# A hybrid decoder step in which the build-time scheduling pass is given another timing model

## The chip, the cores and the metric

One of the eight cores of a Trainium2 chip runs the whole step as one program. The metric is device time in microseconds (us), the median of several runs; a profiled execution gives the trace. TensorE multiplies matrices, VectorE (DVE) and ScalarE (ACT) do elementwise work, GpSimd (POOL) a little of it, and SyncE (SP) issues most transfers. Each engine takes its own queue of instructions in the order in which it was written.

## The reference

Two layers run over 320 tokens (256 of a prompt, 64 of eight sample sequences), with 1024 features, everything in float32:

```python
def layer(x, p, lw, h0, cache_k, cache_v):
    x = x + 0.5 * swiglu(rms_norm(x, lw['ffn1_norm']), ...)      # 1024 -> 2816 -> 1024
    mix, new_k, new_v, h_last = token_mixer(rms_norm(x, lw['mix_norm']), lw, h0, cache_k, cache_v)
    x = x + mix
    x = x + 0.5 * swiglu(rms_norm(x, lw['ffn2_norm']), ...)
    gate = jax.nn.sigmoid((rms_norm(x, lw['ple_norm']) @ lw['ple_w_gate']).astype(F32))
    x = x + ((p @ lw['ple_w_proj']).astype(F32) * gate).astype(x.dtype)

def token_mixer(h, lw, h0, cache_k, cache_v):
    z = h @ lw['w_in']                       # -> u (512) | q (512) | k (128) | v (128)
    y_ssm, h_last = ssm_scan(u, h0, ...)     # h_t = Abar h_{t-1} + Bbar u_t, 32 groups, 64 complex states each
    y_attn = attn_prompt(...) or attn_sample(...)   # window of 128 keys, one sink for each head
    y = jnp.concatenate([rms_norm(y_ssm, ...), rms_norm(y_attn, ...)], axis=-1)
    return y @ lw['w_out'], new_k, new_v, h_last
```

A final RMSNorm follows. The new keys and values and the last states are outputs too.

## The kernel before

Features lie on the 128 partitions, tokens along the rows, so the residual `x` is eight tiles of 128x320. A float32 product is done as three products of rounded parts (`mm3`, L177 to L187): weight and operand are each split into a rounded half (`wh`, `xh`) and a remainder (`wl`, `xl`), and L181, L182 and L183 accumulate wh*xh, wh*xl and wl*xh. One weight block of 1024 columns thus gives 24 matmuls against eight feature blocks.

Weights come in one long order (`weight_order`). `wfetch` loads a block through SP into one of four `wr` buffers (L158), ScalarE rounds it into `wh` (L162), VectorE subtracts to get `wl` (L163); there are four buffers of `wh` and of `wl` (`WB`). `wtake` keeps two blocks fetched ahead (`PF`) in the source.

A layer is a feed-forward part (`ffn`: gate and up products, L287 to L295, down products, L326 to L337), the token mixer (`mix`), a second `ffn` and the layer-input part (`ple`). In layer 0 the tables of the state-space scan for both layers are made beside the two `ffn` (`prep`), and `step` holds these instructions behind a recent weight split, a recent GpSimd instruction and a recent transfer with `tc.issue_after`.

The mixer's units are written in the order that `MIXSEQ` lists: `p` are projections (L577; evacuated by VectorE at L596, L600 or L603), `i` turns a quarter of u into chunks (L607: transposes L613 and L618, products L624, with copies by ScalarE between), `h` is the scan on VectorE (L647 to L685: steps `astep` at L639 to L645, the fix-up at L678 to L683), `v` transposes the values (L701), `s`, `f` and `m` are scores (L725 for the prompt), transposes (L750) and value products (L759) of attention, `y` are the outputs of the scan (L844, L855), `z` the layer-input projections, which need nothing of the mixer, `t` and `w` load tables of the scan (L567), `g` is a gate product, `A` and `S` the output projections. In the middle it reads

```python
... i1 p8 h0 t1 p9 v t2 p5 t0 e x p4 y0 s0 s1 w2 f0 p6 m0 p7 s2 f1 t3 m1 s3 f2 m2 y0 w3 y0 y1 s4 ...
```

That source order is not yet the order of the queues. When the `with _tile.TileContext(...)` block in `_build` closes, a scheduling pass plays the traced program against a model of the machine. As soon as an engine is free in the model it is given, of the instructions that are ready there (inputs made, a buffer of their pool free), the one that comes first in the source. The order found in this way is written out as the engine's queue and stays fixed on the chip. Named edges such as those of `issue_after` are kept.

Of the kernel before, what the change touches and what calls it, by code (L numbers as in the profile page):

```python
# [49 lines left out]
def hybrid_step_kernel(ctx: ExitStack, tc, I, O):  # L50
    nc = tc.nc
# [14 lines left out]
    def nm(s):  # L66
        uid[0] += 1
        return f"{s}_{uid[0]}"
# [7 lines left out]
    def pst(tag):  # L76
        return pp_.tile([P, 512], F32, name=nm(tag), tag=tag, bufs=PBUFS[tag])
# [4 lines left out]
    def cp(out, in_):  # L82
        S.activation(out, in_, AF.Copy)

# [1 line left out]
    ident = cpool.tile([P, P], F32, name="ident")  # L86
    make_identity(nc, ident)
    ones = cpool.tile([P, 1], F32, name="ones")
# [18 lines left out]
    def gcol(l, off, m):  # L107
        c = l * NPRM + off + m
        return prm[:, c : c + 1]

# [1 line left out]
    seq = MIXSEQ.split()  # L112
    def weight_order():
        for l in range(L):
# [72 lines left out]
                    waiting.pop(0)[1]()  # L187

    class Norm:
        """Statistics and split operand of an RMSNorm over nb feature blocks."""  # L190

        def __init__(self, nb, gain, split=True, pre=1.0):
            self.nb, self.gain, self.split, self.pre = nb, gain, split, pre
# [41 lines left out]
            ]  # L235

        def finish(self, then=None):
            """Statistics of the row scale; its broadcast is left for later, behind a few products."""
            ps = pst("pa")
            for c, t0 in enumerate(STAT):  # L240
                sums = [self.acc] + self.sums
                for i, a in enumerate(sums):
                    PE.matmul(ps[:SN, c : c + 1], a[:, t0 : t0 + SN], ones, start=i == 0,
                              stop=i == len(sums) - 1)
            ms = sm.tile([SN, 3], F32, name=nm("ms"), tag="ms", bufs=2)
            V.tensor_scalar(ms, ps[:SN, :3], 1.0 / (self.nb * P), EPS, op0=OP.mult, op1=OP.add)  # L246
            r4 = sm.tile([SN, 3], F32, name=nm("r4"), tag="r4", bufs=2)
            lastpool.append(PO.tensor_tensor(r4, ms, mhalf, op=OP.pow).ins)  # L248
            if then is None:
                return self.spread(r4)  # L250

            def later():
                pr = self.spread(r4)
                r = sm.tile([P, T], F32, name=nm("r"), tag="r", bufs=2)
                if self.pre == 1.0:
                    V.tensor_copy(r, pr)
                else:
                    V.tensor_scalar(r, pr, self.pre, None, op0=OP.mult)
                then(r)

            waiting.append([LATER, later])
# [5 lines left out]
                             ident[:SN, :SN])  # L267
            return pr[:, :T]

# [1 line left out]
    def ffn(l, idx, pre, post, side=None, after=3):  # L271
        xs = pre.pairs()
        r = None
# [62 lines left out]
                    post(mo)  # L336
                step(side)  # L337

# [1 line left out]
    wb_d = [dram.tile([4, P, 1024], F32, name=f"wbd{l}") for l in range(L)]  # L340
    wc_d = [dram.tile([4, P, 1024], F32, name=f"wcd{l}") for l in range(L)]
    kt_d = [dram.tile([512, P], F32, name=f"ktd{l}") for l in range(L)]
# [210 lines left out]
            PO.dma_start(dst[:, :, i * 16 :], src[:, :, : (8 - i) * 16])  # L553
            yield

# [1 line left out]
    def mix(l, pre, post):  # L557
        xs = pre.pairs()
        rr = []
# [15 lines left out]
        kv = []  # L575
# [133 lines left out]
                   qT[pz, :, TP:T].rearrange("p m (b i) -> p m b i", i=8))  # L709

        class Prompt:
            """Block m of the query heads (one head of each kv head) over both query blocks."""

            def __init__(self, m):
                self.m = m
# [38 lines left out]
            def mix(self):  # L754
                po = pst("po")
                for n in (1, 0):
                    for kb in range(n + 1):
                        for k in range(2):
                            PE.matmul(po[k * 64 : k * 64 + 64, n * P : (n + 1) * P],  # L759
                                      vtok[:, kb, k * 64 : k * 64 + 64],  # L760
                                      self.pt[:, 2 * n + kb * 2 + k, :], start=kb == 0, stop=kb == n)
                cp(ya[:, self.m, 0:TP], po[:, 0:TP])

        class Sample:
            """Four of the sample sequences."""

            def __init__(self, tp):
                self.tp = tp
# [159 lines left out]
        PO.dma_start(O["kcs"][l], kct[:, :, 8:P])  # L928
        PO.dma_start(O["vcs"][l], vct[8:P])

# [1 line left out]
    pj_now = {}  # L932

    def ple_load(l):
# [44 lines left out]
            while r is not None and pend:  # L979
                gate(*pend.pop(0))  # L980

# [1 line left out]
    pre = Norm(8, lambda m: gcol(0, GF1, m))  # L983
    nc.sync.dma_start(xa[:, 0:2], I["xT"][:, 0:2])
    nc.sync.dma_start(prm, I["prm"])
# [13 lines left out]
    for l in range(L):  # L999
        nmix = Norm(8, lambda m: gcol(l, GMIX, m))  # L1000
        ffn(l, 1, pre, lambda m: nmix.add(m, x[m]), side if l == 0 else None,
            FAFTER[0] if l == 0 else FAFTER[1])
        if l == 0:
            for _ in side:
                pass
        nf2 = Norm(8, lambda m: gcol(l, GF2, m))
        mix(l, nmix, lambda m: nf2.add(m, x[m]))
        nple = Norm(8, lambda m: gcol(l, GPLE, m))
        side = prep(1) if l == 0 else None
        ffn(l, 2, nf2, lambda m: nple.add(m, x[m]), side, FAFTER[2])  # L1010
        if side is not None:
            for _ in side:
                pass
        if l + 1 < L:
            pre = Norm(8, lambda m: gcol(l + 1, GF1, m))
        else:
            pre = Norm(8, None, split=False)
        ple(l, nple, lambda m: pre.add(m, x[m]))
# [7 lines left out]
        (nc.sync if i % 2 == 0 else S).dma_start(O["yT"][:, m0:m1], y)  # L1026


# [1 line left out]
def _blocks(w, mper, kper=None):  # L1030
    n, k, m = w.shape
    a = w.reshape(n, k // P, P, m // (P * mper), mper, P)
    a = a.transpose(0, 3, 2, 4, 1, 5)
    return a.reshape(n, m // (P * mper), P, mper * (k // P) * P)
# [75 lines left out]
def _build(arrays):  # L1110
    import concourse.bacc as _bacc
    import concourse.tile as _tile

    nc = _bacc.Bacc("TRN2", target_bir_lowering=False, num_devices=1)
    I = {
        n: nc.dram_tensor(n, a.shape, mybir.dt.from_np(a.dtype), kind="ExternalInput").ap()
        for n, a in arrays.items()
    }
    O = {n: nc.dram_tensor("o_" + n, s, F32, kind="ExternalOutput").ap() for n, s in _OUTS.items()}
    with _tile.TileContext(nc) as tc:  # L1120
        hybrid_step_kernel(tc, I, O)
    return nc

# [26 lines left out]
```

## Time and profile before

| | us |
|---|---|
| median of 3 runs | 1305.47 |
| lowest and highest | 1303.61, 1311.94 |
| profiled execution, its span | 1307.1 |
| TensorE busy in it | 1272.5 |
| VectorE busy | 894.7 |
| ScalarE busy | 599.1 |

The profile is of one execution. Busy time of TensorE counts matmuls whose ends are modelled, so it tells when the engine lacked work and not how fast it worked; the granted clock stands beside it (1.00 is 2.4 GHz, 0.50 is 1.2 GHz). A wait is idle time of an engine just before an instruction, with the instruction that ended it.

### The profile page before, as it was taken

Reading aid. Unit: us, or ns where it says so; the run is one execution under the profiler, and the core shown is the slowest. Engines: PE = TensorE matmul, PEld = TensorE weight load, DVE = VectorE, ACT = ScalarE, POOL = GpSimd, SP = SyncE. Lnnn points to the kernel's source line nnn. Section 1 sums busy time; section 2 is a strip of 40 time slices with the busy share of each in tenths; the row PEclk is TensorE's granted clock in tenths of the full one; section 3 lists DMA queues with packets and bytes.
Section 4 is the critical chain, followed back from the end, with each engine's and each line's share of the span. In section 5 each row is a group of like instructions: output and inputs, shape, how many; then the busy total and the mean of one; then the engine's idle time right before and its main releaser. Section 6 shows DMA issues by size and latency. Waiting matters only on the chain.

```text
span 1307.1 us, 22973 instructions
## 1 busy us (share of the span) xinstructions
PE 1272.5 (97%) x9153; PEld 1241.5 (95%) x9153; DVE 894.7 (68%) x1583; ACT 599.1 (46%) x986; POOL 72.7 (6%) x92
## 2 busy tenths in 40 slices
PE   7999999998999999999999999999899999999996
PEld 7999999987899999999999999999778999999996
DVE  6588885758896978656875555566778755555575
ACT  5433434543864443334653334345357544334453
POOL 4300001000004000100000000000000000000000
PEclk9999999997999999999999999999979999999998
DMA  7836766652254467754554455345322444454351
GB/s 259 307 115 202 249 208 206 194 168 84 76 179 146 138 209 252 233 180 137 169 172 146 125 165 162 123 138 185 130 81 84 147 147 140 134 178 147 110 179 41
DMA packets 74619, 210.62 MB, mean 161 GB/s; under 512 B 8544, under 2 KB 18496, under 8 KB 74480
## 3 DMA queue, kind: packets, MB, share of 16 engines
q1 hardware_dynamic: 72560, 203.22, 48.6%
q0 software_dynamic: 1664, 5.28, 1.2%
q8 instruction: 72, 1.18, 0.4%
q10 hardware_dynamic: 288, 0.66, 0.1%
q14 instruction: 35, 0.29, 0.1%
HBM read 191.78 MB, written 19.69 MB: 162 GB/s over the span
## 4 chain that ended last, share of the span: by engine, by line
PE 91%; DVE 5%; issue 2%; ACT 0%; DMA 0%; POOL 0%; SPq 0%; POOLq 0%; DVEq 0%
PE pt L181 17%; PE pt L183 17%; PE pt L182 17%; PE pc L181 10%; PE pc L183 10%; PE pc L182 10%; PE pa L844 1%; DVE sc L641 1%; DVE wl L163 1%; PE pa L624 1%; PE pa L613 1%; PE pt L725 1%; PE pa L499 1%; PE pt L750 0%; DVE sc L644 0%
## 5 line engine op out<-in xcount | busy, mean ns | idle before, releaser
L162 ACT ACTIVATE wh<-wr 128x1024 fp32r<-128x1024 f32 (+3 forms) x365 | 351.1, 963 | 562.1 <-issue 284.0
L181 PE MATMUL pt<-big,wh 128*128 128x320 f32 x1584 | 491.6, 311 | 1.0 <-ACT big L228 1.0
L182 PE MATMUL pt<-big,wh 128*128 128x320 f32 x1584 | 490.8, 310 | 0.0
L183 PE MATMUL pt<-big,wl 128*128 128x320 f32 x1584 | 490.5, 310 | 0.2 <-DVE wl L163 0.2
L163 DVE TENSOR_TENSOR wl<-wr,wh 128x1024 fp32r<-128x1024 f32 (+3 forms) x365 | 403.4, 1108 | 111.8 <-ACT wh L162 110.2
L181 PE MATMUL pc<-big,wh 128*128 128x320 f32 x992 | 314.0, 317 | 6.8 <-ACT wh L162 5.9
L183 PE MATMUL pc<-big,wl 128*128 128x320 f32 x992 | 310.4, 313 | 0.0
L182 PE MATMUL pc<-big,wh 128*128 128x320 f32 x992 | 310.3, 313 | 0.0
L181 PEld LDWEIGHTS pt<-big,wh 128*128 128x128 f32 x1584 | 297.8, 188 | 2.0 <-ACT big L228 1.5
L183 PEld LDWEIGHTS pt<-big,wl 128*128 128x128 f32 x1584 | 297.7, 188 | 0.8 <-DVE wl L163 0.6
L182 PEld LDWEIGHTS pt<-big,wh 128*128 128x128 f32 x1584 | 297.9, 188 | 0.4
L181 PEld LDWEIGHTS pc<-big,wh 128*128 128x128 f32 x992 | 188.9, 190 | 11.3 <-ACT wh L162 5.9
L182 PEld LDWEIGHTS pc<-big,wh 128*128 128x128 f32 x992 | 189.1, 191 | 1.4 <-DVE big L225 1.2
L183 PEld LDWEIGHTS pc<-big,wl 128*128 128x128 f32 x992 | 188.9, 190 | 0.8 <-DVE wl L163 0.4
L290 DVE TENSOR_TENSOR fa<-pt,ft 128x320 f32<-128x320 f32 x88 | 43.1, 490 | 98.1 <-PE pt L183 97.9
L287 DVE TENSOR_TENSOR ft<-pc,r 128x320 f32<-128x320 f32 x88 | 42.9, 490 | 58.5 <-PE pc L183 58.4
L248 POOL TENSOR_TENSOR r<-ms,mhalf 107x3 f32<-107x3 f32 x13 | 13.4, 1032 | 734.8 <-DVE ms L246 734.8
L333 DVE SCALAR_TENSOR_TENSOR fd<-pt,r 128x320 f32<-128x320 f32 x64 | 31.4, 490 | 32.8 <-PE pt L183 32.8
L294 ACT ACTIVATE big<-fa 128x320 fp32r<-128x320 f32 x88 | 40.5, 460 | 20.0 <-DVE fa L290 19.7
L288 ACT ACTIVATE ft<-ft 128x320 f32<-128x320 f32 x88 | 40.0, 457 | 19.9 <-DVE ft L287 19.9
L224 ACT ACTIVATE big<-xa,prm 128x320 fp32r<-128x320 f32 x64 | 35.3, 559 | 22.7 <-DVE xa L334 9.8
L295 DVE TENSOR_TENSOR big<-fa,big 128x320 fp32r<-128x320 f32 x88 | 42.7, 485 | 2.7 <-ACT big L294 2.7
(236 smaller groups left out, 893.6 us busy)
## 6 DMA issues: line engine op xcount, KB each, us to landing
wr<-f1u SPq DMA_DIRECT2D x44, 512.0 KB, 3.4
wr<-f2g SPq DMA_DIRECT2D x44, 512.0 KB, 3.4
wr<-f2u SPq DMA_DIRECT2D x44, 512.0 KB, 3.3
wr<-f1g SPq DMA_DIRECT2D x43, 512.0 KB, 3.4
wr<-f1d SPq DMA_DIRECT2D x32, 384.0 KB, 3.2
wr<-f2d SPq DMA_DIRECT2D x32, 384.0 KB, 3.2
wr<-f1d SPq DMA_DIRECT2D x32, 320.0 KB, 2.9
wr<-win SPq DMA_DIRECT2D x20, 512.0 KB, 4.0
```

What stands on the lines that cost most here:

```text
L162: S.activation(h[:, c], raw[:, c], AF.Copy)
L163: i = V.tensor_tensor(lo[:, c], raw[:, c], h[:, c].bitcast(F32), op=OP.subtract)
L181: PE.matmul(ps, h[:, c], xh, start=start and k == 0, stop=False)
L182: PE.matmul(ps, h[:, c], xl, start=False, stop=False)
L183: PE.matmul(ps, lo[:, c], xh, start=False, stop=stop and k == n - 1)
L224: S.activation(h, src, AF.Copy, scale=g)
L287: V.tensor_tensor(t, pg, r, op=OP.mult)
L288: S.activation(t, t, AF.Silu)
L290: V.tensor_tensor(a, pu, t, op=OP.mult)
L294: S.activation(h, a, AF.Copy)
L295: V.tensor_tensor(lo, a, h.bitcast(F32), op=OP.subtract)
L333: V.scalar_tensor_tensor(t, pd, 0.5, r, op0=OP.mult, op1=OP.mult)
```

## The change

The scheduling pass is asked to play the program against a second, finer model: one that keeps a timeline of events for every device (an engine's sequencer, its waits, its datapath, the transfer queues) in place of the default machine model. The pass, its priorities, the pools and the source are the same. The other hunks remove comments and docstrings (`# ---- constants ----` and the like); one stands for them here.

```diff
@@ -82,7 +82,7 @@
     def cp(out, in_):
         S.activation(out, in_, AF.Copy)
 
-    # ---- constants ----
+
     ident = cpool.tile([P, P], F32, name="ident")
...
@@ -1117,7 +1117,7 @@
     O = {n: nc.dram_tensor("o_" + n, s, F32, kind="ExternalOutput").ap() for n, s in _OUTS.items()}
-    with _tile.TileContext(nc) as tc:
+    with _tile.TileContext(nc, schedule_with_timeline_sim=True) as tc:
         hybrid_step_kernel(tc, I, O)
     return nc
```

## Rows read from the trace of the kernel before

**Rows 1.** Page, busy us (share of the span) and instructions of each engine

```profile
PE 1272.5 (97%) x9153; PEld 1241.5 (95%) x9153; DVE 894.7 (68%) x1583; ACT 599.1 (46%) x986; POOL 72.7 (6%) x92
```

**Rows 2.** Stages: window length, busy (x) of PE PEld DVE ACT POOL, clock, DMA, GB/s

```profile
0.00:14.00 14.00, 6.97 (x19) 4.89 (x20) 7.62 (x9) 8.00 (x14) 8.00 (x17) 1.00 0.81 284
14.00:258.00 244.00, 244.00 (x1706) 241.84 (x1706) 184.26 (x340) 106.69 (x153) 24.81 (x26) 1.00 0.66 214
258.00:362.00 104.00, 95.92 (x860) 84.01 (x859) 74.96 (x167) 56.81 (x134) 7.79 (x14) 0.93 0.33 109
...
898.00:1003.00 105.00, 96.41 (x851) 84.32 (x850) 73.63 (x166) 56.35 (x133) 5.25 (x10) 0.92 0.30 101
1003.00:1262.00 259.00, 259.00 (x1773) 258.67 (x1772) 157.01 (x233) 112.09 (x167) 2.65 (x2) 1.00 0.47 147
1262.00:1307.10 45.10, 34.17 (x237) 33.65 (x236) 28.07 (x50) 20.24 (x36) 1.70 (x2) 0.89 0.21 75
```

**Rows 3.** Waits of TensorE: line <- releaser, us in total, times, longest us

```profile
PE pt L725 <- DVE big L600: 5.6, 2, 2.8
PE pa L844 <- DVE big L683: 5.3, 2, 2.9
PE pt L701 <- DVE kv L603: 3.0, 2, 1.5
```

**Rows 4.** Narrow windows around the scans of both layers, columns as in rows 2

```profile
296.00:301.70 5.70, 2.92 (x21) 2.27 (x19) 5.55 (x15) 1.06 (x1) 0.00 (x0) 0.93 0.27 92
301.70:308.00 6.30, 6.25 (x25) 5.68 (x26) 5.36 (x18) 0.09 (x1) 0.00 (x0) 0.52 0.27 86
314.80:322.00 7.20, 7.19 (x42) 5.61 (x43) 5.58 (x11) 1.78 (x5) 0.95 (x2) 0.54 0.15 46
...
940.50:947.00 6.50, 6.04 (x32) 5.83 (x33) 6.07 (x21) 1.06 (x1) 0.00 (x0) 0.74 0.25 83
953.20:968.00 14.80, 14.71 (x93) 12.09 (x93) 10.33 (x21) 5.84 (x21) 1.15 (x3) 0.55 0.34 117
```

**Rows 5.** Timeline of TensorE, layer 0: start, us, line, out<-in, count, [idle before <-releaser]

```profile
264.78 1.03 PE L613 MATMUL pa<-ident,big 128*40 128x128 f32 x8 [0.16 <-DVE big L596]
...
288.56 0.31 PE L183 MATMUL pc<-big,wl 128*128 128x320 f32 x1
290.35 0.55 PE L701 MATMUL pt<-ident,kv 128*128 128x128 f32 x3 [1.48 <-DVE kv L603]
...
298.61 0.31 PE L183 MATMUL pc<-big,wl 128*128 128x320 f32 x1
301.75 1.23 PE L725 MATMUL pt<-kv,big 64*128 64x256 f32 x4 [2.82 <-DVE big L600]
...
314.81 0.65 PE L844 MATMUL pa<-wc,big 128*40 128x128 f32 x4 [2.39 <-DVE big L683]
```

**Rows 6.** VectorE at the scan of layer 0: windows, timeline, groups; last, ScalarE's casts

```profile
258.00:285.00 27.00, 26.69 (x295) 23.84 (x295) 9.84 (x12) 13.41 (x22) 2.62 (x4) 1.00 0.52 171
285.00:315.00 30.00, 23.31 (x149) 21.51 (x147) 27.30 (x69) 7.57 (x11) 0.72 (x2) 0.88 0.27 89
...
285.83 0.29 DVE L657 COPY big<-big 128x128 f32<-128x128 f32 x1 [3.74 <-ACT big L83]
314.20 0.56 DVE L683 TENSOR_TENSOR big<-big,s 128x384 f32<-128x384 f32 x1
...
L163 DVE TENSOR_TENSOR wl<-wr,wh 128x1024 fp32r<-128x1024 f32 x3 | 3.7, 1230 | 0.0
L600 DVE TENSOR_TENSOR big<-pc,r 128x320 f32<-128x320 f32 x3 | 1.5, 488 | 0.6 <-PE pc L183 0.6
L162 ACT ACTIVATE wh<-wr 128x1024 fp32r<-128x1024 f32 x5 | 5.3, 1061 | 16.2 <-PE pc L182 14.5 <-PE pt L182 1.6
```

**Rows 7.** SP's timeline; then transfers by line, count, KB each, us to landing

```profile
297.22 6.17 SPq L158 DMA_DIRECT2D wr<-woa  x2
...
tt<-ttd SPq DMA_DIRECT2D x8, 512.0 KB, 4.6
```

## The prediction

> **What bounds the kernel now.** I read the page's busy shares first, then a table of windows by stage, the waits of TensorE, the clock in narrow windows, and the timelines of TensorE, VectorE and SP around the widest gaps. By the shares [rows 1] TensorE is busy 1272.5 of 1307.1 us and so lacks work for 34.6 us. The stage table [rows 2] says where. In the long dense stretches (three: 14 to 258, 362 to 898 and 1003 to 1262 us; the first and the last are shown) busy equals the window: 244 + 536 + 259 = 1039 us without idle time. Their pace is 259.00 us / 1773 = 0.146 us for a matmul of 320 columns, so a group of 24 (eight feature blocks, three products each) takes 3.5 us. No order makes these shorter. What is left is the head (7.0 us idle in the first 14), the two mixers (104.00 - 95.92 = 8.1 and 105.00 - 96.41 = 8.6 us) and the tail (10.9 us in the last 45.1). The granted clock is 1.00 in the dense stretches, 0.93 and 0.92 in the mixers.
>
> Inside the mixers the waits [rows 3] are few: 5.6 us for the queries' evacuation (L600), 5.3 us for the last add of the scan (L683), 3.0 us for the value's evacuation (L603), each in both layers. Most are followed by the lower of the two clock levels [rows 4]: after the 2.82 us wait that ends at 301.75 [rows 5] the mean granted clock is 0.52 for 6.3 us, after the wait that ends at 314.81 it is 0.54 for 7.2 us, and in layer 1 0.55 for 14.8 us. Taking 1.2 GHz as 0.5 and 2.4 GHz as 1.0, a window of length w and mean c spent 2(1-c)w at the low level: 0.8 + 6.0 + 6.6 = 13.4 us in layer 0 and 3.4 + 13.3 = 16.7 us in layer 1, 30 us in all.
>
> The timeline [rows 5] shows the cause. TensorE takes its queue in order. It runs nine matmuls of a projection, the last at 288.56, then sits 1.48 us before L701, with the rest of the same projection queued behind it. At 298.61 it leaves another projection in the middle for the first scores (L725), which wait 2.82 us for L600; the rest comes after the scores. The queue was laid out for evacuations that come sooner. They are late because VectorE is full: 27.30 of 30.00 us from 285, and 9.84 of 27.00 before [rows 6]. Its chain runs from L657 at 285.83 to the first L683 at 314.20, 28.4 us; in it stand three weight splits of 1.23 us and three evacuations of 0.49 us that aren't scan steps.
>
> **The change part by part.** The removed comments and docstrings compute nothing: zero. The argument to `TileContext` adds no instruction, transfer or tile. It changes the times by which the pass judges what is ready, hence the order in each engine's queue. That the order hangs on such times is seen in [rows 5]: `MIXSEQ` has s0 ahead of p6, and the scores stand in the middle of that projection.
>
> *Dense stretches*: 0. TensorE is never short of a weight there; the largest VectorE share is 184.26 of 244.00 us [rows 2], so an evacuation or split that moves by a place is hidden under 3.5 us of matmuls. If that cover went, a late weight would cost its split, 1.2 us, once for each stretch: bounds 0 and +4.
>
> *Head and tail*: 0. The head starts with nothing loaded, the tail has nothing behind it to fill with. Bounds: a split's time either way, 1.2 us.
>
> *Mixers*: a finer model can see that L701 and L725 aren't ready and let the rest of the projection through. That fills 1.48 + 2.82 = 4.3 us per layer. But the matmuls that fill it leave the cover behind: after the scores there are projections until the wait for L683 (2.39 us, ending at 314.81), and this wait grows by as much, since the scan sets its end. Only work that now runs after the scan is a real filler. The second half of the layer-input projection is (z4 to z7: four times two blocks times three products, 24 matmuls, 3.5 us), and its weight needs a split of 1.23 us on the full VectorE. Net 3.5 - 1.2 = 2.3 us per layer, 4.6 in both. From below: 0, if the order stays. From above: all three waits in both layers, 13.9 us, and the low clock. I take the value near the lower end, because VectorE ends last here and no step of its chain goes away: -4.5 us.
>
> Of the low clock I count nothing back. Of the 6.3 us at 0.52 VectorE is busy 5.36 [rows 4], so matmuls at full pace would there mostly reach the wait for L683 sooner. A rule of the Trainium skill ("TensorE: Matmul & The Clock Gate", Terms) puts the penalty at the throttled time times the share of pulses left out, here one half: by it 15 of the 30 us are loss, and an order that keeps the clock up would bring the sum to 1287 in place of the one below. The VectorE row is why that is a rival and not the forecast.
>
> *Sum*: 1307.1 - 4.5 = 1302.6 us of span. The median of the runs shown, 1305.5, lies 1.6 below that span, so 1301 for the median. One per cent is 13 us, about what a measurement of this kernel can tell from no change.
>
> **The rivals.**
>
> *Faster, the scan set free.* The three splits (3.7 us) and three evacuations (1.5 us) fall ahead of the scan, where VectorE is a third busy [rows 6], and it ends 5.2 us sooner. With the low clock shortened by half (which gives back a quarter of its time) this is 5.2 + 3.4 us in layer 0 and 5.2 + 4.2 in layer 1, 18 in all: 1287. For it: the waits at L701 and L725 are misjudged readiness. Against: a split needs one of four buffers (`WB`), and in this stretch the casts wait 14.5 us for matmuls that still hold one [rows 6].
>
> *Faster, the clock kept up.* The same work with no gap that lets the clock fall: half of 30 us, 15, so 1290. [...] Against: the VectorE row above.
>
> *Slower, the cover spent too early.* From 264.78 (L613) to 285.83 the projections share TensorE with the transposes that feed the scan, 21.1 us. If the finer model finds the transposes ready later and puts one more group of 24 ahead of two of the four chains, the scan starts 7.0 us later and the same 7.0 us are missing under it. The wait of 2.39 us becomes 9.4, and the low clock lasts longer: 13.3 us as in layer 1 against 6.0 is 7.3 us at half pace, 3.6 us. Some 10.6 per layer, 21 in both: 1327. It decides from two groups per layer on (4 x 3.5 = 14 us). For it: filling takes whatever is ready, and TensorE now waits only 0.16 us at L613, so nothing forces the present share. Against: the chains come early in source order.
>
> *Slower, a table behind weights.* SP issues in order; from 297.22 two weight loads in a row span 6.17 us, and a table (`tt`) takes 4.6 us to land [rows 7]. A table queued behind such a pair makes L844 wait up to 10.8 us, less the 2.4 that it waits anyway: 8.4 per layer, 17 in both, 1322.
>
> *No change.* Both models lead to nearly the same queues: 1305.
>
> **How the numbers follow.** The small trim at 1301 has 0.38, and its own range is 1293 to 1311: all 8.6 us of L701 and L725 gained against the bounds +4 and +1.2 and no trim. No change 0.07. Scan set free 0.17, clock kept up 0.08. Cover spent early 0.20, table late 0.10. So faster by over 1% 0.25, within it 0.45, slower 0.30. The range 1284 to 1330 holds the centres of all cases; out of it stay the far end of the faster ones (1305.5 - 13.9 - 15 = 1277) and a slower one with a third group misplaced (1327 + 7 = 1334), together some 2 in 10.
>
> **What would show it.** Right: the dense stretches free of idle time at 0.146 us a matmul; the waits at L701 and L725 smaller and the one at L844 larger; L657 to the first L683 within 2 us of 28.4. Scan set free: fewer than three L163 in that chain, and the chain shorter by 4 us or more. Clock kept up: 0.97 or more over a whole mixer. Cover spent early: L613 to L657 3 us longer than 21.1, and a wait for L683 over 5 us. Table late: L844 released by a transfer. All of it is wrong if waits appear inside a dense stretch, for instance a split queued behind an evacuation that waits for TensorE: at 0.3 us in each of the 88 feed-forward blocks (four times 22) that would be 26 us.

## The result: the finer model's order starts the scan 24 us later in each layer

The changed kernel takes 1362.76 us (median of 4 runs, 1361.26 to 1364.68) against 1306.97 us of the kernel before on the same chip: a ratio of 1.043, 95% interval 1.041 to 1.045, so 56 us slower. The forecast was 1301 with a range of 1284 to 1330; it was wrong in size and in sign.

The page's busy shares of the changed kernel, as in [rows 1]:

```profile
PE 1273.1 (94%) x9153; PEld 1244.5 (92%) x9153; DVE 897.1 (66%) x1583; ACT 600.4 (44%) x986; POOL 79.2 (6%) x92
```

Instructions and busy times are those of [rows 1]. The span is 1359.5 us, 52.4 more, and TensorE lacks work for 1359.5 - 1273.1 = 86.4 us in place of 34.6: 51.8 more. The whole loss is time in which TensorE has nothing to do. The table of windows (columns as in [rows 2]) says where:

```profile
258.00:300.00 42.00, 42.00 (x355) 40.06 (x354) 18.68 (x24) 19.34 (x29) 3.33 (x4) 1.00 0.44 149
300.00:360.00 60.00, 32.80 (x347) 27.21 (x347) 43.00 (x110) 23.07 (x68) 1.56 (x5) 0.74 0.20 67
360.00:420.00 60.00, 53.41 (x382) 50.53 (x379) 41.66 (x80) 33.72 (x71) 4.11 (x5) 0.89 0.28 96
430.00:660.00 230.00, 230.00 (x1622) 228.39 (x1621) 176.10 (x331) 99.55 (x144) 17.04 (x18) 1.00 0.60 192
926.00:968.00 42.00, 42.00 (x368) 39.88 (x366) 18.91 (x24) 20.39 (x32) 3.29 (x4) 1.00 0.45 150
968.00:1030.00 62.00, 34.89 (x329) 28.17 (x326) 45.14 (x114) 22.96 (x70) 1.56 (x5) 0.70 0.18 60
1100.00:1300.00 200.00, 200.00 (x1366) 200.00 (x1365) 111.53 (x157) 79.09 (x115) 0.00 (x0) 1.00 0.45 144
```

The dense stretches are free of idle time and keep their pace (200.00 / 1366 = 0.146 us a matmul). The first 42 us of each mixer are full too (in the kernel before TensorE was busy for 39.1 and 38.3 of the 42 us from 258 and from 898). Then TensorE idles 27.2 of 60 us in layer 0 and 27.1 of 62 in layer 1. What it waits for (columns as in [rows 3]):

```profile
PE pa L844 <- DVE big L683: 42.2, 2, 21.1
PE pa L844 <- DMA tt<-ttd: 8.3, 2, 4.2
PE pa L266 <- POOL r L248: 6.8, 3, 4.1
PE pa L243 <- DVE acc L215: 4.1, 1, 4.1
```

The 5.3 us of [rows 3] for the last add of the scan are now 42.2. The waits at L701 and L725 are gone from the list. Timelines of layer 0, TensorE, then ScalarE, then VectorE (start, us; columns as in [rows 5]):

```profile
270.65 1.03 PE L613 MATMUL pa<-ident,big 128*40 128x128 f32 x8
...
275.27 0.68 PE L618 MATMUL pa<-ident,sx 40*128 40x40 f32 x8
...
313.64 0.66 PE L844 MATMUL pa<-tt,big 128*40 128x128 f32 x4 [4.07 <-DMA tt<-ttd]
335.43 0.65 PE L844 MATMUL pa<-wc,big 128*40 128x128 f32 x4 [21.14 <-DVE big L683]
```

```profile
271.28 1.07 ACT L83 ACTIVATE sx<-pa 40x512 f32<-40x512 f32 x2 [1.97 <-PE pa L613]
...
304.93 1.23 DVE L163 TENSOR_TENSOR wl<-wr,wh 128x1024 fp32r<-128x1024 f32 x1 [4.70 <-ACT wh L162]
310.09 0.28 DVE L657 COPY big<-big 128x128 f32<-128x128 f32 x1 [3.93 <-ACT big L83]
```

ScalarE's copies of the first chunk end at 271.28 + 1.07 = 272.35, but the transposes that need them (L618) start at 275.27, since 25 dense matmuls (products of 320 columns, L181 to L183) stand between them in TensorE's queue (7 before). So it is at every hop (from TensorE through a copy by ScalarE back to TensorE) but the last, where none stand. The windows from the first L613 to the last L624, in the kernel before and in the changed one, show the sum:

```profile
264.70:285.30 20.60, 20.38 (x251) 17.75 (x251) 6.14 (x7) 10.86 (x19) 0.56 (x1) 1.00 0.55 180
```

```profile
270.60:309.60 39.00, 38.43 (x378) 35.47 (x376) 12.68 (x16) 19.62 (x35) 1.53 (x3) 1.00 0.46 158
```

The chain itself is 192 matmuls in both. Counted in the order of the trace, the rest is 58 dense matmuls before and 169 after, to which the changed kernel adds 15 of L701, L725 and L727. The 111 more dense ones are 111 x 0.146 = 16.2 us, the other 15 take about 2, together the 18.3 us by which L613 to L657 grew (21.1 to 39.4). The first L613 is 5.9 us late as well (L266 comes 3.0 us later, and 22 more dense matmuls, 3.2 us, stand between it and L613; in all 41 more dense matmuls run ahead of it, 41 x 0.146 = 6.0 us). So L657 starts 24.3 us later, at 310.09 against 285.83 [rows 6].

The sum for layer 0: L657 is 24.3 us late; the chain from L657 to the first L683 is 24.7 us in place of 28.4, 3.7 shorter, as no L163 and no L600 stands in it any more; the first L683 is 20.6 us late. To this come 5.7 us more of idle time in the 40 us behind the mixer (6.6 against 0.9; the waits at L243 and L266 above). That is 26.3 us. Layer 0 lost 26.5 and layer 1 25.5, read from the starts of the same dense matmuls behind each mixer.

### The profile page after: what moved, and what is told of

It is laid out like the page before. It is cut to its first block, busy times and chain, and to the rows that moved or that the text cites. A ratio compares the mean times of both kernels' runs of the same rounds, so it can differ in the third digit from the quotient of the medians.

```text
span 1359.5 us, 22987 instructions
## 1 busy us (share of the span) xinstructions
PE 1273.1 (94%) x9153; PEld 1244.5 (92%) x9153; DVE 897.1 (66%) x1583; ACT 600.4 (44%) x986; POOL 79.2 (6%) x92
## 4 chain that ended last, share of the span: by engine, by line
PE 88%; DVE 6%; issue 3%; ACT 1%; DMA 1%; POOL 0%; SPq 0%; POOLq 0%; DVEq 0%; ACTq 0%
PE pt L181 17%; PE pt L182 17%; PE pt L183 17%; PE pc L181 11%; PE pc L182 10%; PE pc L183 10%; PE pa L844 1%; DVE sc L641 1%; PE pa L624 1%; PE pt L725 1%; DVE wl L163 1%; PE pt L750 1%; PE pa L613 1%; PE po L759 1%; DVE sc L639 1%
## 5 line engine op out<-in xcount | busy, mean ns | idle before, releaser
L163 DVE TENSOR_TENSOR wl<-wr,wh 128x1024 fp32r<-128x1024 f32 (+3 forms) x365 | 403.4, 1106 | 163.4 <-ACT wh L162 159.9
L181 PE MATMUL pt<-big,wh 128*128 128x320 f32 x1584 | 490.9, 311 | 1.5 <-ACT big L228 1.5
L182 PE MATMUL pt<-big,wh 128*128 128x320 f32 x1584 | 491.0, 310 | 0.6 <-DVE big L229 0.6
L183 PE MATMUL pt<-big,wl 128*128 128x320 f32 x1584 | 490.6, 310 | 0.3 <-DVE wl L163 0.2
L181 PE MATMUL pc<-big,wh 128*128 128x320 f32 x992 | 309.7, 314 | 7.5 <-ACT wh L162 5.6
L183 PE MATMUL pc<-big,wl 128*128 128x320 f32 x992 | 308.3, 311 | 0.8 <-DVE wl L163 0.8
L182 PE MATMUL pc<-big,wh 128*128 128x320 f32 x992 | 308.2, 311 | 0.0
L181 PEld LDWEIGHTS pt<-big,wh 128*128 128x128 f32 x1584 | 298.6, 189 | 2.2 <-ACT big L228 1.7
L182 PEld LDWEIGHTS pt<-big,wh 128*128 128x128 f32 x1584 | 298.4, 188 | 1.1 <-DVE big L229 1.1
L183 PEld LDWEIGHTS pt<-big,wl 128*128 128x128 f32 x1584 | 298.3, 188 | 1.0 <-DVE wl L163 0.9
L181 PEld LDWEIGHTS pc<-big,wh 128*128 128x128 f32 x992 | 187.2, 189 | 11.0 <-ACT wh L162 5.6
L183 PEld LDWEIGHTS pc<-big,wl 128*128 128x128 f32 x992 | 187.2, 189 | 1.3 <-DVE wl L163 1.2
L182 PEld LDWEIGHTS pc<-big,wh 128*128 128x128 f32 x992 | 187.1, 189 | 1.3 <-DVE big L225 0.8
L248 POOL TENSOR_TENSOR r<-ms,mhalf 107x3 f32<-107x3 f32 x13 | 21.5, 1657 | 770.9 <-DVE ms L246 770.9
L844 PE MATMUL pa<-wc,big 128*40 128x128 f32 x128 | 18.2, 332 | 42.2 <-DVE big L683 42.2
L844 PEld LDWEIGHTS pa<-wc,big 128*40 128x40 f32 x128 | 11.4, 140 | 43.9 <-DVE big L683 43.0
L294 ACT ACTIVATE big<-fa 128x320 fp32r<-128x320 f32 x88 | 40.2, 459 | 16.4 <-DVE fa L290 16.2
```

Source lines behind the costliest of these rows:

```text
L163: i = V.tensor_tensor(lo[:, c], raw[:, c], h[:, c].bitcast(F32), op=OP.subtract)
L181: PE.matmul(ps, h[:, c], xh, start=start and k == 0, stop=False)
L182: PE.matmul(ps, h[:, c], xl, start=False, stop=False)
L183: PE.matmul(ps, lo[:, c], xh, start=False, stop=stop and k == n - 1)
L294: S.activation(h, a, AF.Copy)
L844: PE.matmul(py[e * 64 : e * 64 + NC, g2 * P : (g2 + 1) * P], src[:, gb * 8 + g8, :], w[:, g8, :], start=first, stop=not first)
```

## The experiments

All kernels here compute the whole step; what differs is the order of queues. The program is traced twice. The first trace, under one model (`ORDER_BY`), gives each engine's order; in the second, under a model of its own (`REST_BY`; `True` is the finer one), the instructions of the engines in `PINNED` are held to that order by edges without a semaphore:

```diff
+            for a, b in zip(order, order[1:]):
+                tc.add_manual_dep(t[b], t[a].name, mybir.DependencyInfo(
+                    mybir.DependencyClass.NoSync, mybir.DependencyReason.DATA), reason="pin")
-    with _tile.TileContext(nc) as tc:
+    with _tile.TileContext(nc, schedule_with_timeline_sim=fine) as tc:
```

The queues that aren't pinned are laid anew around the pinned ones, so a run tells of a pinned queue together with what the model makes of it. The runs were made on several chips, on which the kernel before takes 1305.3 to 1309.4 us; each ratio is to its runs on the same chip, and a difference of two medians below is good to a few us. All results together, the ratio with its interval, and from each trace in layer 0 the two legs of the path and the idle time in the 40 us behind the mixer:

| kernel | median, us | ratio (95%) | L613 to L657 | L657 to L683 | idle behind |
|---|---|---|---|---|---|
| before | 1306.97 | 1 | 21.1 | 28.4 | 0.9 |
| after | 1362.76 | 1.043 (1.041 to 1.045) | 39.4 | 24.7 | 6.6 |
| e1: finer, PE of before | 1332.51 | 1.019 (1.016 to 1.022) | 21.1 | 32.8 | 2.8 |
| e2: default, PE of after | 1375.69 | 1.052 (1.048 to 1.056) | 39.7 | 22.6 | 9.1 |
| e3: finer, PE of before in one stretch | 1327.67 | 1.015 (1.012 to 1.019) | 21.1 | 34.3 | 6.8 |
| e4: finer, SP of before | 1374.99 | 1.051 (1.047 to 1.055) | 41.4 | 26.9 | 6.6 |
| e10: finer, DVE of before | 1348.51 | 1.032 (1.029 to 1.035) | 27.2 | 27.1 | 5.0 |
| e5: finer, PE and DVE | 1316.90 | 1.008 (1.007 to 1.010) | 21.0 | 27.9 | 1.8 |
| e11: finer, PE, DVE and ACT | 1304.66 | 0.999 (0.997 to 1.001) | 21.1 | 27.6 | 0.9 |
| e6: default, 48 ahead | 1322.59 | 1.013 (1.010 to 1.015) | 28.4 | 25.8 | 0.9 |
| e7: default, readers late | 1311.06 | 1.004 (1.002 to 1.005) | 21.1 | 28.7 | 0.9 |
| e9: default, 29 behind | 1325.18 | 1.013 (1.011 to 1.016) | 24.7 | 29.1 | 0.9 |
| e12: default, fix-up in one piece | 1305.84 | 1.000 (0.998 to 1.001) | 21.1 | 26.9 | 0.9 |
| e13: after, gaps cut, DVE of after | 1366.10 | 1.045 (1.043 to 1.048) | 39.6 | 24.8 | 6.6 |
| e14: after, gaps cut | 1343.18 | 1.026 (1.023 to 1.028) | 25.4 | 28.8 | 6.8 |

### Which queue carries the loss

Theory A: TensorE's order carries it, by the matmuls ahead of the chain. Rivals: the order of SP (a late table), or those of the engines that feed the scan.

**e1.** `PINNED = ("PE",)`, `ORDER_BY = False`, `REST_BY = True`.

> The finer model, but the queue of TensorE alone is held to the order that it had before; the other queues are laid out by the finer model around it. Theory A (the loss is TensorE's order: the chains that feed the scan stand behind projections): 1300 to 1316 us, the scan of layer 0 starts near 286 us, the wait of L844 for L683 is below 5 us a layer. Theory B (the loss comes from the queues of VectorE, ScalarE or SP): above 1340 us.

1332.51 us: between the two. TensorE's old order takes 30 of the 56 us back, and L613 to L657 is 21.1 us again. But the scan's own chain grew to 32.8. The groups of VectorE in it (line, tiles, count, busy us and mean ns) and the wait behind it in layer 0:

```profile
L163 DVE TENSOR_TENSOR wl<-wr,wh 128x1024 fp32r<-128x1024 f32 x5 | 6.1, 1224 | 0.1
...
L600 DVE TENSOR_TENSOR big<-pc,r 128x320 f32<-128x320 f32 x4 | 2.0, 488 | 0.0
```

```profile
PE pa L844 <- DVE big L683: 12.3, 1, 12.3
```

Five weight splits and four evacuations stand among the scan's steps, where [rows 6] has three of each, so VectorE's order has a share of its own.

**e2.** The counterpart: `PINNED = ("PE",)`, `ORDER_BY = True`, `REST_BY = False`.

> The mirror image: the default model, but the queue of TensorE alone held to the order that the finer model gave. Theory A: 1345 to 1370 us, with the scan of layer 0 near 310 us and a wait of L844 near 20 us a layer. Theory B: below 1320 us.

1375.69 us, above what was expected and worse than the changed kernel. TensorE's new order alone is enough for the late scan (39.7 us). Of the 19.8 us by which its profiled span (1379.3) exceeds that of the changed kernel, 5.3 are idle time of TensorE and 14.6 its busy time (1287.7 against 1273.1), at a lower granted clock (0.951 against 0.964); what lowers the clock there isn't shown.

**e3.** As e1, but TensorE is held only from the first L613 to the last L624 of each mixer, and what came later stays behind.

> The finer model, with TensorE's queue held to the old order only from the first L613 to the last L624 of each mixer, and what came behind that stretch kept behind it; all else is free. Theory A: the scans start near 286 us and 925 us, 1305 to 1320 us in all. Theory C (TensorE's order after the scan matters as much): 1325 to 1345 us.

1327.67 us (1.015, interval 1.012 to 1.019), by its time inside theory C. Still, e1, in which the whole queue of TensorE is that of before, is no faster, so TensorE's order behind the stretch isn't the rest, and what e1 wins back is won in this one stretch. The rest shows elsewhere: the scan's chain is 34.3 us here.

**e4.** `PINNED = ("SP",)`, `ORDER_BY = False`, `REST_BY = True`.

> The finer model, with SP's queue alone held to the order of before, so that the table tt is issued as early as it was. If the waits for that table (8.3 us in two) are on the path: 1352 us. If, as theory A has it, they only come ahead of a longer wait for the scan: 1357 to 1365 us, with the wait for the table gone and that for L683 longer by as much.

1374.99 us, outside both. The waits of TensorE:

```profile
PE pa L844 <- DVE big L683: 45.2, 2, 22.6
PE pa L844 <- DMA tt<-ttd: 9.5, 2, 4.8
```

The old order of SP doesn't bring the table sooner and delays more elsewhere. So this run doesn't test an earlier table. In the changed kernel the products of the table start at 313.64, 21 us ahead of the scan's end, so by its timeline the wait costs nothing there.

**e5.** `PINNED = ("PE", "DVE")`, `ORDER_BY = False`, `REST_BY = True`.

> The finer model, with the queues of TensorE and VectorE held to the order of before; ScalarE, GpSimd and SP laid out by the finer model. In the run with TensorE alone held, five weight splits stood in the scan's chain on VectorE in place of three, and the first L683 came 32.8 us after L657 in place of 28.4. Theory D (what is left there, 24 us, is VectorE's order): 1303 to 1316 us, L657 to the first L683 28 to 29 us. Rival (ScalarE's or SP's order): 1320 us or more.

1316.90 us, just above the first. VectorE's order is worth 1332.5 - 1316.9 = 15.6 us more. About 10 us stayed open.

**e10.** VectorE alone: `PINNED = ("DVE",)`.

> The finer model's queues, VectorE's alone put back to the order of the kernel before. If the two queues cost independently, VectorE's part is what it was with TensorE's order restored, 15.6 us: 1347. If VectorE's order only matters once TensorE's is restored (because the scan now waits for the transposes and VectorE has time), nothing is gained: 1357 to 1366. If the orders of the two must match, the mixed pair is worse than either: over 1370.

1348.51 us, the additive figure. It isn't additive by mechanism, though: with VectorE held, the pass also laid TensorE's queue anew, with 82 dense matmuls inside the chain in place of 169, and L613 to L657 fell to 27.2 us.

**e11.** `PINNED = ("PE", "DVE", "Activation")`.

> The finer model, with the queues of TensorE, VectorE and ScalarE put back. With TensorE and VectorE alone 1316.9 was left, 10.6 over the kernel before. If ScalarE's casts and copies are the rest: 1304 to 1310. If it is GpSimd's or SP's order (transfers): 1314 to 1319 as without it.

1304.66 us, the kernel before. By the medians ScalarE's order is the last 12 us, but the two profiles don't show these as waiting: TensorE's idle time is 39.3 us in e5 and 38.6 in e11, its busy time 1275.8 and 1263.4, at a granted clock of 0.985 and 0.993. So a part of the 12 us is clock. At 0.985 two runs of e5 took 1316.9 and 1319.0 us and one of e11 1309.3, which leaves some 8 us for ScalarE's order; whether that order also moves the clock isn't shown. Against the profile of the kernel before, which has the same clock of 0.985, e5 has 4.7 us more idle time, in small waits (2.9 us in all for ScalarE's copies ahead of L759, and 1.8 us in place of 0.9 behind the mixer). With three queues restored, SP and GpSimd may stay as the finer model lays them around the three: their order costs nothing.

### What a matmul ahead of the chain costs

**e6.** Default model, TensorE pinned to its own order with 24 more dense matmuls ahead of the second chunk and 24 more ahead of the fourth, the dose of the prediction's slower rival:

```diff
+            late = {"i2": 24, "i1": 48}.get(ks[k], late)
+            mine = ks[k] in ("i0", "i1", "i2", "i3", "o", "c")
+            out.append((dense + late * mine, ks[k] == "d", k))
```

> The default model and the queue of TensorE as before, but in each mixer 24 more dense matmuls stand ahead of the second chunk's transposes and 24 more ahead of the fourth's, 48 in all; the order among the dense matmuls is kept. This is the dose of the slower rival of the prediction. By that rival: scan 7.0 us later, 10.6 us lost per layer, 21 in all, 1329 us. By the slope of the changed kernel (26 us lost per layer for a scan 24 us later): 7.0 us later, 7.6 lost per layer, 1323 us. If a late scan were harmless up to the wait it has now: below 1315.

1322.59 us, as the slope has it: 16.3 us above the 1306.34 of the kernel before on the same chip, 8.1 per layer for 48 x 0.146 = 7.0. L613 to L657 grew by 7.4 (28.42 against 21.05). The wait it turned into:

```profile
PE pa L844 <- DVE big L683: 16.7, 2, 8.4
```

**e9.** The other direction: the 29 dense matmuls between the second chunk's first transposes and the last product of the chunks go behind that product.

```diff
+        start = next(k for k in range(end - 420, end) if ks[k] == "i2")
+        part = list(range(start, end + 1))
+        order[start : end + 1] = [order[k] for k in part if ks[k] != "d"] + [
+            order[k] for k in part if ks[k] == "d"]
```

> The default model's queues, but the 29 dense matmuls that stand between the second chunk's first transposes and the last chunk's products go behind those products, in each mixer. It is the dose of the earlier run with the sign turned. If the slope holds on this side too (the scan starts by as much earlier as dense time is taken from ahead of it), 29 x 0.146 = 4.2 us per layer, 8.5 in both: 1298 against 1306.5, with L613 to L657 down from 21.1 to 17 us and the idle time of the scan from 6.7 to about 3. If ScalarE's copies between the hops (about 3.4 us for a chunk, one chunk every 4.4 us now) set the chain's pace, the matmuls taken out leave holes: L613 to L657 shrinks by less than 2 us and the time stays within 1304 to 1310.

1325.18 us: neither, 18 us slower. The timeline of TensorE in layer 0, then in layer 1, and windows over both (columns as in [rows 2]):

```profile
276.38 1.90 PE L613 MATMUL pa<-ident,big 128*40 128x128 f32 x8
278.96 1.07 PE L618 MATMUL pa<-ident,sx 40*128 40x40 f32 x8 [0.68 <-ACT sx L83]
280.56 1.94 PE L624 MATMUL pa<-big,wb 128*64 128x40 f32 x32 [0.53 <-ACT big L83]
...
925.17 1.22 PE L613 MATMUL pa<-ident,big 128*40 128x128 f32 x8
927.07 0.68 PE L618 MATMUL pa<-ident,sx 40*128 40x40 f32 x8 [0.68 <-ACT sx L83]
928.28 1.13 PE L624 MATMUL pa<-big,wb 128*64 128x40 f32 x32 [0.53 <-ACT big L83]
```

```profile
276.40:288.60 12.20, 9.78 (x99) 7.71 (x97) 0.00 (x0) 4.12 (x9) 0.00 (x0) 0.50 0.28 87
903.00:934.10 31.10, 27.12 (x300) 24.08 (x299) 10.53 (x14) 14.79 (x26) 1.15 (x2) 1.00 0.48 156
```

A hop without filling leaves TensorE idle for 0.68 and 0.53 us: this is the copy through ScalarE, and it is what 4 or 5 matmuls of 0.146 us cover. The kernel before has 4 to 7 in most gaps, so taking them away speeds the chain by only 0.5 us in layer 1 (L613 to L657 20.5 against 21.0). In layer 0 the clock fell to 0.50 at 275.3, behind the first two of the same six gaps, and the chain became 3.6 us longer. The 29 matmuls then came late: a projection behind them was evacuated (L600) only after the scan's fix-up, and TensorE waited 6.4 us for it in each layer. A gap wants as many matmuls as its hop lasts, and the changed kernel has 12 to 25 in most of them.

### Two queues that hold the scan together

**e13.** The finer model's own order for TensorE and VectorE, with one edit in TensorE's: from the second chunk's first transposes on at most 5 dense matmuls stay in a gap (`CAP`); what is over, and the scores, go behind the chain. Of 169 dense matmuls 83 stay inside the chain, 48 of them in its first three gaps. The other three queues are laid anew.

> The finer model's own queues of TensorE and VectorE, with one edit in TensorE's: from the second chunk's first transposes on, at most 5 dense matmuls stay in each of the eight gaps of the transposes' chain, where the changed kernel has 18, 24, 11, 20 and four times 12; the other 80 or so and the scores go behind the chain (the other three queues are laid anew). By the slope of the dose run, about 80 x 0.146 + 1.9 for the scores = 13.6 us per layer, 27 in both: 1335 against 1362.8, with L613 to L657 at 26 us instead of 39.4. If VectorE's queue of the changed kernel, with weight splits ahead of L657 whose operands now come later, holds the scan back instead, L657 waits for a split's cast and not for the last product of the chunks, L613 to L657 stays over 33 us and the time over 1348.

1366.10 us: the chain is repaired and nothing is won. TensorE's last products, VectorE's first step, and the wait:

```profile
294.97 1.13 PE L624 MATMUL pa<-big,wb 128*64 128x40 f32 x32 [0.53 <-ACT big L83]
```

```profile
300.95 0.49 DVE L600 TENSOR_TENSOR big<-pc,r 128x320 f32<-128x320 f32 x1 [6.46 <-PE pc L183]
...
305.42 1.22 DVE L163 TENSOR_TENSOR wl<-wr,wh 128x1024 fp32r<-128x1024 f32 x1 [0.46 <-ACT wh L162]
309.69 1.23 DVE L163 TENSOR_TENSOR wl<-wr,wh 128x1024 fp32r<-128x1024 f32 x1 [3.05 <-ACT wh L162]
310.83 0.29 DVE L657 COPY big<-big 128x128 f32<-128x128 f32 x1
```

```profile
PE pa L844 <- DVE big L683: 47.6, 2, 23.8
```

The last products end at 296.1 in place of 309.6, but L657 still starts at 310.83, without a wait of its own: VectorE's queue has a wave of weight splits and evacuations ahead of it. These wait for dense matmuls that TensorE now runs later: the evacuation (L600) directly, the split through ScalarE's cast, which itself waits for dense matmuls (L182; 4.2 and 2.5 us ahead of the casts that start at 300.81 and 304.33).

**e14.** The same edit, VectorE's queue laid anew too.

> The same edit of TensorE's queue as in the run before (at most 5 dense matmuls in the later gaps of the chain), but VectorE's queue isn't held to that of the changed kernel: the pass lays it anew around the edited queue. If the two queues hold the scan back together (in the run before the chain ended 13 us sooner and L657 still started at 310.83, behind two weight splits), L613 to L657 falls to 24 to 28 us and the wait at L844 to under 16 us: 1328 to 1342. If the late scan comes from something that neither queue holds (a transfer, a buffer), it stays late: over 1355.

1343.18 us, 1 us above what was expected. L657 starts at 296.84, released by the copy of the last products, and L613 to L657 is 25.4 us:

```profile
296.84 0.29 DVE L657 COPY big<-big 128x128 f32<-128x128 f32 x1 [2.13 <-ACT big L83]
```

The first L683 is 9.2 us sooner than in the changed kernel (325.6 against 334.8), twice this is 18.4, and the span fell by 18.6. So TensorE's order suffices to start the scan late (e2), with that order edited VectorE's queue holds it as late (e13), and the scan comes free when both change (e14). This fits e1 and e10, whose free queues were laid anew around the pinned one and which win more than the edit of one queue in e13.

### The prediction's own step, and a try to win

**e7.** Default model; L701 and the first L725 go behind the projection that they split.

> The default model and the queue of TensorE as before, but the value transposes (L701) and the first scores (L725) stand behind the whole projection that they split in two, in both layers, so that the waits of 1.48 and 2.82 us there have ready matmuls to run. The prediction's step says that this gains next to nothing, since the wait for L683 grows by as much: 1303 to 1309 us, that wait 4 to 7 us a layer in place of 2.4 to 2.9. If the waits were a loss of their own: 8.6 us less, 1298 us.

1311.06 us (1.004, interval 1.002 to 1.005), 2 us above what was expected: the waits that ended at L701 and L725 (1.48 and 2.82 us in [rows 5]) fell to nothing and 1.1 us, and came back at L844, 8.8 us a layer and so more than the 4 to 7 expected:

```profile
PE pa L844 <- DVE big L683: 17.5, 2, 8.8
```

More than these waits came back. TensorE's busy time fell by 3.6 us (1272.5 to 1268.9): it was busy for 21.4 us at the low clock in place of 30.3. Its idle time rose by 5.8 (34.6 to 40.4). So the clock that was won also ended in the wait for the scan, which has four weight splits in its chain here in place of three.

**e12.** Default model; on VectorE alone the first half of the fix-up runs ahead of the second.

> The default model's queues; on VectorE alone the first half of the scan's fix-up (four steps and L683) runs ahead of the second half, which the kernel before mixes in (two of its steps, 0.82 + 0.79 = 1.6 us, stand ahead of the first L683 at 314.20). If the end of the scan sets the end of the mixer, as every run so far says, the wait of 2.4 us at the first L844 shrinks to about 0.8 in each layer: 3.2 us less, 1303.5. If the second half, now 1.6 us later behind an add that was moved up, is what the scores and the other L844 wait for: within 1 us of the kernel before.

1305.84 us (1.000, interval 0.998 to 1.001), the second of the two outcomes. The line numbers below stand one higher than in the kernel before:

```profile
PE pt L726 <- DVE s L729: 3.5, 2, 1.7
...
PE pa L845 <- DVE big L684: 2.4, 2, 1.5
```

The wait for the scan fell from 2.65 to 1.2 us a layer, and 1.7 us came up at the scores, whose mask add (L728 of the kernel before) is what now comes late on VectorE. No version was found that beats the kernel before.

## Why the prediction was wrong, step by step

- **What bounds the kernel**: right. The dense stretches kept 0.146 us a matmul without idle time, and everything happened in the mixers and just behind them. *Dense stretches*, *head and tail* at zero: right within 1 us (the tail by 0.1); the 4.1 us that VectorE's `acc` (L215) makes L243 wait lie behind a mixer and were not priced.
- **Mixers**: the step that failed. It took the readers at L701 and L725 to move and the scan to start where it did. They did move and their waits are gone, as the step says, but e7 shows that this alone is worth nothing (1311). The step was right that the scan's end decides, and wrong that the scan's start is fixed: the finer model's order puts it 24.3 us later in each layer, the wait for L683 grows from 2.65 to 21.1 us, and the term of -4.5 us became a loss of 52. The step's bound on the side of a loss was zero; the order of the transposes' chain was put only into a rival. The lower end of the small trim's own range is also off by its own figures: 8.6 us off the 1305.5 of no change is 1297, not 1293.
- **Rival "cover spent too early"** (0.20, 1327): this is what happened. L613 to L657 grew, the wait for L683 passed 5 us, as its marks asked. Its price for a matmul was near (10.6 us per layer for 48; e6 measured 8.1), its dose was not: 111 dense matmuls and 15 others inside the chain and 41 ahead of it, 167 in place of 48. It also knew only one queue. VectorE's own order, which e13 shows to hold the scan as late, and ScalarE's (some 8 us at the same clock) weren't in it.
- **Rival "scan set free"**: its mechanism came too. The chain from L657 to L683 is free of splits and 3.7 us shorter, against 5.2 in that rival. They moved ahead of the scan, where they are part of the queue that holds L657 as soon as the transposes' chain is repaired (e13); in the changed kernel itself L657 waits for that chain. Two more steps of the fix-up (L680, L681) now stand ahead of the first L683 and take back some of the 5.2.
- **Rival "table behind weights"**: its mark came (L844 released by a transfer, 4.2 us in each layer), without a cost: the scan ends 21 us later anyway.
- **The low clock**: the prediction gave nothing back for it, and for this change that was right. The mean granted clock of the two profiled runs is 0.985 before and 0.964 after, by the prediction's formula 39 and 98 us at the low level, and TensorE's busy time grew by 0.6 us. The Trainium skill ("TensorE: Matmul & The Clock Gate", Terms) puts the penalty at the throttled time times the share of pulses left out, which would be 29 us more than before; the trace does not agree, since most of the added low clock lies on time in which TensorE had nothing to run (from 312.7 to 340.0, at 0.50, it was busy for 5.2 of 27.3 us). In the kernel before, where 30.3 of 40.2 us at the low level lie on work, the time does follow the clock: on one chip three runs of the kernel before at a mean clock of 0.983 took 1312.2 to 1312.6 us, five at 0.993 took 1303.4 to 1305.0. As to the rival "clock kept up", e7 won 3.6 us of busy time and lost it again in the wait for the scan.

Open: why the finer model fills the gaps with 12 to 25 matmuls. The chip's traces show what the order does, not what the model took a hop to last. Where ScalarE's share lies, and how much of the 12 us between e5 and e11 is the clock, is read from runs at the same clock and not shown by an edit.

## What to carry to other kernels

Where one engine's queue carries both a dependent chain and its filler, read the idle time that a hop leaves when nothing fills it, and let no more filler stand in a gap than covers it: every matmul more moved the chain's end by about its own length here (7.4 us for 48 in e6). A scheduling model that shows a fuller engine early can be a slower one, since the filler spent there is missing under the longest wait. And before blaming one queue, look whether a second one would hold the same step just as late: an edit of one of two such queues can gain nothing by itself (e13).

## What the hardware showed beyond that

The same gaps of 0.5 to 0.7 us between short matmuls in e9 left the granted clock at 1.00 in layer 1 and at 0.50 for 17.1 us in layer 0 (275.3 to 292.4, from behind the second gap on); at 0.50 eight L613 took 1.90 us in place of 1.22 and 32 L624 1.94 in place of 1.13. What the engine did ahead of the fall was the same in both layers to about a hundredth of a microsecond, so nothing in these rows tells the two apart. The Trainium skill ("TensorE: Matmul & The Clock Gate", Part 1) says of the clock's rise that its point varies from run to run for the same matmuls. This trace shows a fall, and it differs between two like stretches of one run.
